# Ordering the recurrence's gate products in a hybrid attention and recurrent layer: a fixed place, a fixed alternation, and an early sigmoid

## The chip, the cores and the metric

The kernel runs on one core of one Trainium2 chip. A core has a matrix engine (PE, TensorE), whose weight loads are shown as an engine of their own (PEld), and four other engines: DVE (VectorE), ACT (ScalarE), POOL (GpSimd) and SP (SyncE, which here issues DMA transfers). Each engine works through its own list of instructions in order, and waits for another engine through semaphores. The metric is the device time of one execution in microseconds (us). Less is better. Where several timed executions of a kernel are given, their median is compared.

## The reference

One decoder layer, 1024 tokens with 16 learned meta tokens ahead of them, 1024 features, all in float32. The input is normalised, and one projection gives five parts: queries, keys and values of an attention with a window of 128 tokens, and two inputs, x and y, of a recurrence over 512 channels. The two results are joined and projected out, normalised and added to the input; a feed-forward part with squared ReLU follows, again normalised and added.

The part that matters here is the recurrence. After a causal convolution of x over 4 tokens:

```python
xb = x.reshape(bsz, t, LRU_BLOCKS, LRU_BLOCK)          # 8 blocks of 64 channels
gate_r = einsum("btnc,ncd->btnd", xb, w_a) + b_a
gate_i = einsum("btnc,ncd->btnd", xb, w_x) + b_x
r, i = sigmoid(gate_r), sigmoid(gate_i)
log_a = -LRU_C * r * softplus(-lam)
a = exp(log_a);  mult = sqrt(-expm1(2 * log_a))
h_t = a_t * h_(t-1) + mult_t * i_t * x_t
rec = gelu(y) * h
mix = concat([attention, rec]) @ w_out
```

So the gates are products with small block-diagonal matrices, of 64 by 64 each; each sigmoid needs its whole gate product; the exponential, the square root and the scan over time follow the sigmoids; and the output projection needs the attention for its first 512 input features and the recurrence for the other 512.

## The kernel before

Every float32 matrix product is done as three products of numbers cut to a shorter mantissa: each operand is split into a high part (a cast, on ACT, line 96) and a low part (the rest, a subtraction on DVE, line 99), and high by high, high by low and low by high are summed in one PSUM bank. The function `mm3` (lines 125, 130, 131) issues the three. A product of 128 rows by 512 columns is the common case.

The kernel goes through the layer in this order. It projects keys, values and the first queries. It then runs eight steps of attention (`scores` and `attend`, four pairs of blocks of tokens for each of two groups of heads). Ten further projections, the `fills` (queries, x and y of the recurrence), give PE products to run while the softmax and the splits go on elsewhere: eight are emitted one a step, with a priority lowered by `FILL_LAG`, and the last two, the y projections of channel blocks 2 and 3, behind the gates in the source (the products L125, L130 and L131 into a bank `ps_acc` that the trace shows between the gates are such projections). After the attention come the gates of the four channel blocks, 128 channels each; then the rest of the recurrence in two halves, blocks 0 and 1 and then blocks 2 and 3; then the output projection, the norm and the feed-forward part.

The gates (`gates(c)`) work as follows. A block of 128 channels holds two of the reference's blocks of 64. Each gate product uses 64 of PE's 128 rows: for s = 0 the one half of the rows, for s = 1 the other. The 1040 tokens go in three thirds of 348, 348 and 344 columns. For each third there are two PSUM banks, one for each s, taken in turn from three rings of banks (`s`, `pt`, `o`), and six matmuls, three for each s (line 819). So a block has 18 gate matmuls and the four blocks 72. Two sigmoids a third (through `lut`, line 82) read the banks into z. The rings are shared with other work: the `o` banks are the value banks of `attend` (matmuls of line 697, read by a copy on ACT, line 706, and an addition on DVE, line 707), and a bank is free for its next use only when its readers are done.

Behind the gates, `gather` (lines 833 to 836) puts the halves together and multiplies by x; `decay` takes exponentials and tanh; `recur` takes a square root and then two multiplications and a scan on DVE (lines 851, 852, 853); `rec_out` (line 858) multiplies by gelu(y) and splits the result into the operands of the output projection, `at[half][2]` for blocks 0 and 1 and `at[half][3]` for blocks 2 and 3. `split_wo` splits the output weights. `out_mm` then runs the output projection, eight input chunks kc of 128 features: kc 0 to 3 read the attention, kc 4 and 5 the recurrence's blocks 0 and 1, kc 6 and 7 its blocks 2 and 3. Later, `u2_tiles` transposes a normalised tile of tokens on PE (line 1003) and scales it out of PSUM (ACT line 1014, DVE line 1008); `combine` (line 1029) forms the sums and differences that the feed-forward's fast matrix scheme multiplies; line 96 splits them.

The order in which an engine runs its instructions isn't that of the source. A list scheduler takes the whole program, with priorities by place in the source and a model of times, and writes out one list for each engine. Three helpers bind it by order alone, without a semaphore: `lut` chains every table function on ACT in source order, because a change of function set costs a table load (line 82, ACT_TABLE_LOAD); `chained` does the same for chosen splits; and `behind(name, ins)` makes one instruction come after another in the order:

```python
def behind(name, *inss):
    for ins in inss:
        tc.add_manual_dep(ins, name, mybir.DependencyInfo(
            mybir.DependencyClass.NoSync, mybir.DependencyReason.DATA), reason="order")
```

Nothing binds the gate matmuls before the change: the scheduler puts each where it finds it ready.

Of the kernel before, what the change touches and what calls it, by code (L numbers as in the profile page):

```python
# [9 lines left out]
F32 = mybir.dt.float32  # L10
F32R = mybir.dt.float32r
AF = mybir.ActivationFunctionType
ALU = mybir.AluOpType
# [3 lines left out]
P = 128  # L17
# [20 lines left out]
def hybrid_layer(  # L38
# [6 lines left out]
    nc = tc.nc  # L45
# [4 lines left out]
    small = ctx.enter_context(tc.tile_pool(name="small", bufs=4))  # L50
# [4 lines left out]
    bufs = {"raw": 2, "ws": 5, "a": 16, "b": 17, "c": 8, "d": 4, "e": 2}  # L55
    uid = [0]

    def slot(tag, shape, dt=F32):
        uid[0] += 1
        return slab.tile(shape, dt, tag=tag, name=f"{tag}{uid[0]}", bufs=bufs[tag])  # L60

    def pair(tag, shape):
        return slot(tag, shape, F32R), slot(tag, shape, F32R)

    def bank(tag, shape=(P, 512)):
        uid[0] += 1
        return ps.tile(list(shape), F32, tag=tag, name=f"ps_{tag}{uid[0]}")

    def f32(ap):
        return ap.bitcast(F32)  # L70
# [8 lines left out]
    last_lut = [None]  # L79

    def lut(*args, **kwargs):
        ins = nc.scalar.activation(*args, **kwargs).ins
        if last_lut[0] is not None:
            tc.add_manual_dep(
                ins, last_lut[0],
                mybir.DependencyInfo(
                    mybir.DependencyClass.NoSync, mybir.DependencyReason.DATA
                ),
                reason="lut",
            )  # L90
        last_lut[0] = ins.name
        return ins

    def split(hi, lo, src, eng=None):
        if eng is None:
            nc.scalar.copy(hi, src)  # L96
        else:
            eng.tensor_copy(hi, src)
        low = nc.vector.tensor_tensor(lo, src, f32(hi), op=ALU.subtract).ins  # L99
        mark[0] = low.name  # L100
        return low
# [4 lines left out]
    def behind(name, *inss):  # L106
        for ins in inss:
            tc.add_manual_dep(
                ins, name,
                mybir.DependencyInfo(  # L110
                    mybir.DependencyClass.NoSync, mybir.DependencyReason.DATA
                ),
                reason="order",
            )
# [69 lines left out]
    eps_col = const.tile([P, 1], F32, name="eps_col")  # L184
# [346 lines left out]
    for h in range(2):  # L531
        r, o, m = HALF[h], HALF[1 - h], slice(P - NMETA, 2 * P)
# [77 lines left out]
    def scores(jp, quarter):  # L610
# [57 lines left out]
            )  # L668
        return sn

    def attend(jp, quarter, sn):
        flat = sn.rearrange("p a b c -> p (a b c)")
        pp = []
        for h in range(2):

            ph, pl = (slot("c", [P, 4, 2, P], F32R) for _ in range(2))
            pt = bank("pt")
            for i in range(4):
                nc.tensor.transpose(pt[:, i * P : (i + 1) * P], sn[:, h, i, 0:P], ident)
            pt = pt.rearrange("p (a b) -> p a b", a=4)  # L680
            split(ph[:, :, 0], pl[:, :, 0], pt)
            for p_ in (ph, pl):
                for s, g, op in ((1, 1, ALU.is_ge), (0, -1, ALU.is_gt)):
                    nc.gpsimd.affine_select(  # L684
                        out=p_[:, :, s], in_=f32(p_[:, :, 0]), pattern=[[0, 4], [g, P]],
                        compare_op=op, fill=0.0, base=0, channel_multiplier=-g,
                    )
            pp.append((ph, pl))
        kb0 = 2 * quarter
        for h in range(2):  # L690
            po = bank("o")
            two = po.rearrange("p (j c) -> p j c", j=2)
            for n, (oc, pc, w) in enumerate(((0, 0, P), (0, P, 2 * P), (P, 3 * P, P))):
                kb = kb0 + n
                v = vk[h][:, kb - 1, :] if kb else vm[:, h, :]
                for k, p_ in enumerate(pp[h]):
                    nc.tensor.matmul(  # L697
                        two[:, :, oc : oc + w], v,
                        p_.rearrange("p (j i) s c -> p j (i s c)", j=2)[:, :, pc : pc + w],
                        start=n == 0 and k == 0, stop=n == 2 and k == 1,  # L700
                        skip_group_check=True,
                    )

            r, o = HALF[h], HALF[1 - h]
            whole = flat[r, 0:512]
            nc.scalar.copy(whole, po[o, :])
            nc.vector.tensor_tensor(whole, po[r, :], whole, op=ALU.add)
        ah, al = at[quarter // 2][jp]
        c = slice(256 * (quarter % 2), 256 * (quarter % 2) + 256)
        split(  # L710
            ah[:, :, c], al[:, :, c],
            flat[:, 0:512].rearrange("p (j c) -> p j c", j=2),
        )
# [65 lines left out]
    for jp in range(2):  # L779
        at_pair(jp)  # L780
        for quarter in range(4):
            gate_after = last_lut[0]
            sn = scores(jp, quarter)
            with deferred(FILL_LAG):
                next_fill()
            if prev is not None:
                attend(*prev)
            prev = (jp, quarter, sn)
    attend(*prev)


# [10 lines left out]
    nc.vector.tensor_tensor(gw[:, 1], graw, f32(gw[:, 0]), op=ALU.subtract)  # L802

    rg = [None] * NLRU

    def gates(c):
        ch, cl = pair("b", [P, TT])
        split(ch, cl, xc[c])


        z = [slot("c", [P, TT]) for _ in range(2)]
        for t0, n in THIRDS:
            acc = []
            for s in range(2):
                flip[0] += 1
                acc.append(bank(("s", "pt", "o")[flip[0] % 3]))
            for k, (a, b) in enumerate(((0, ch), (0, cl), (1, ch))):
                for s in range(2):
                    nc.tensor.matmul(
                        acc[s][:, :n], gw[HALF[s], a, c, :], b[HALF[s], t0 : t0 + n],  # L820
                        start=k == 0, stop=k == 2, skip_group_check=True,
                    )
            for s in range(2):
                lut(
                    z[s][:, t0 : t0 + n], acc[s][:, :n], AF.Sigmoid,
                    bias=prm[:, c, 5 + s : 6 + s],
                )
        rg[c] = z
# [51 lines left out]
    for c in range(NLRU):  # L880
        gates(c)
        if c < 2:
            gather(c)
# [75 lines left out]
    def out_banks(t):  # L959
        tag = ("pt", "o", "acc", "s", "pt", "acc", "s", "pt")[t]  # L960
        return [bank(tag), bank(tag)]
# [201 lines left out]
    for t in range(8):  # L1163
        po = pos[t] if t < 4 else out_banks(t)
# [396 lines left out]
```

## Time and profile before

| | |
|---|---|
| median of 3 runs | 950.23 us (949.52 to 950.42) |
| profiled execution | 949.03 us |
| its span in the trace | 947.3 us |
| mean granted clock of PE | 0.998 |
| PE busy | 937.9 us, 99% of the span |
| DVE, ACT, POOL busy | 664.4, 505.0, 135.9 us |
| chain that ended last | PE 97%, DVE 1% |
| gate matmuls on PE | from 193.49 to 213.16 us |
| sigmoids on ACT | 24, from 197.31 to 214.58 us |

The table's rows are averages over stages that differ. A row of the timeline gives a start in us from the start of the span, a duration in us, the engine, the line of the kernel, the operation, the tile written and the tiles read, the shape, and how many such instructions were merged into the row; square brackets give how long the engine had been idle before it and what ended that. On PE matmuls overlap in the pipe: the duration of one (0.39 us) is longer than the distance to the next (0.23 us), so costs on PE are taken from distances between starts.

### The profile page before, as it was taken

The numbers are of one execution on the slowest core, as the hardware profiler recorded it, in microseconds if no ns is written. First come the engines' busy times: TensorE is split into PE (matmuls) and PEld (weight loads), VectorE is DVE, ScalarE is ACT, GpSimd is POOL, SyncE is SP. The second block draws the span as 40 slices with busy tenths as digits, with TensorE's granted clock in tenths as the row PEclk, the third lists the DMA queues.
The fourth block names the chain that finished last, engine by engine and source line by source line (L and its number), as shares of the span: only waits on it lengthen the run. The fifth ranks groups of instructions, "written<-read, shape, count | busy, mean of one in ns | idle before, by whom it ended". The sixth has DMA issues, their size and how long they took to land.

```text
span 947.3 us, 12174 instructions
## 1 busy us (share of the span) xinstructions
PE 937.9 (99%) x4584; PEld 784.8 (83%) x4584; DVE 664.4 (70%) x849; ACT 505.0 (53%) x844; POOL 135.9 (14%) x205
## 2 busy tenths in 40 slices
PE   9999999999999999999999999999999999999996
PEld 8999999878888878888888888888888888888885
DVE  6667788779977987665544465476667676779783
ACT  8546765569634664443655575654533443445441
POOL 4104437431021100010000000001111000001201
PEclk9999999999999999999999999999999999999999
DMA  8220011104259658574422363334777655537934
GB/s 273 57 68 23 24 45 45 45 23 141 82 194 273 200 180 283 188 258 134 156 89 89 111 215 120 109 111 114 198 170 178 206 179 192 194 126 209 238 64 89
DMA packets 97366, 134.91 MB, mean 142 GB/s; under 512 B 22230, under 2 KB 61158, under 8 KB 97308
## 3 DMA queue, kind: packets, MB, share of 16 engines
q1 hardware_dynamic: 87996, 108.64, 35.3%
q0 software_dynamic: 8880, 24.19, 11.9%
q10 hardware_dynamic: 432, 1.31, 0.4%
q8 instruction: 36, 0.59, 0.3%
q14 instruction: 22, 0.18, 0.1%
HBM read 112.55 MB, written 20.97 MB: 141 GB/s over the span
## 4 chain that ended last, share of the span: by engine, by line
PE 97%; DVE 1%; DMA 0%; ACT 0%; issue 0%; SPq 0%; DVEq 0%
PE ps_acc L125 12%; PE ps_acc L131 12%; PE ps_acc L130 12%; PE ps_pt L131 6%; PE ps_s L131 6%; PE ps_pt L125 6%; PE ps_pt L130 6%; PE ps_s L125 6%; PE ps_s L130 6%; PE ps_o L125 5%; PE ps_o L131 5%; PE ps_o L130 5%; PE ps_o L697 2%; PE ps_acc L282 1%; PE ps_s L629 1%; PE ps_s L633 1%
## 5 line engine op out<-in xcount | busy, mean ns | idle before, releaser
L99 DVE TENSOR_TENSOR ws<-raw,ws 128x1024 fp32r<-128x1024 f32 (+1 forms) x69 | 82.3, 1193 | 72.4 <-PE ps_o L130 23.1
L96 ACT CAST ws<-raw 128x1024 fp32r<-128x1024 f32 (+1 forms) x68 | 69.8, 1027 | 82.0 <-PE ps_o L130 33.6
L96 ACT CAST ws<-e 128x1024 fp32r<-128x1024 f32 x41 | 43.0, 1050 | 85.8 <-PE ps_o L130 38.2
L130 PE MATMUL ps_acc<-a,ws 128*128 128x512 f32 (+3 forms) x240 | 82.9, 346 | 0.0
L125 PE MATMUL ps_acc<-a,ws 128*128 128x512 f32 (+3 forms) x240 | 82.8, 346 | 0.0
L131 PE MATMUL ps_acc<-a,ws 128*128 128x512 f32 (+3 forms) x240 | 82.2, 343 | 0.0
L99 DVE TENSOR_TENSOR b<-b,b 128x1024 fp32r<-128x1024 f32 (+2 forms) x50 | 59.0, 1179 | 27.9 <-PE ps_o L130 22.6
L99 DVE TENSOR_TENSOR ws<-e,ws 128x1024 fp32r<-128x1024 f32 x41 | 50.2, 1223 | 31.7 <-ACT ws L96 18.4
L96 ACT CAST b<-b 128x1024 fp32r<-128x1024 f32 (+2 forms) x49 | 50.0, 1020 | 41.8 <-DVE b L1029 35.5
L684 POOL TENSOR_SCALAR_AFFINE_SELECT c<-c 128x512 fp32r<-128x512 f32 x64 | 55.0, 873 | 73.7 <-ACT c L96 64.2
L125 PEld LDWEIGHTS ps_acc<-a,ws 128*128 128x128 f32 x240 | 45.2, 189 | 4.3 <-issue 0.7
L131 PEld LDWEIGHTS ps_acc<-a,ws 128*128 128x128 f32 x240 | 45.2, 188 | 3.7 <-issue 0.2
L130 PEld LDWEIGHTS ps_acc<-a,ws 128*128 128x128 f32 x240 | 45.2, 188 | 3.6 <-issue 0.4
L131 PE MATMUL ps_acc<-ws,b 128*128 128x512 f32 (+1 forms) x120 | 46.3, 386 | 0.0
L130 PE MATMUL ps_acc<-ws,b 128*128 128x512 f32 (+1 forms) x120 | 46.2, 385 | 0.0
L125 PE MATMUL ps_acc<-ws,b 128*128 128x512 f32 (+1 forms) x120 | 46.0, 385 | 0.0
L125 PE MATMUL ps_pt<-ws,b 128*128 128x512 f32 x112 | 44.3, 395 | 0.0
L131 PE MATMUL ps_pt<-ws,b 128*128 128x512 f32 x112 | 44.2, 395 | 0.0
L130 PE MATMUL ps_pt<-ws,b 128*128 128x512 f32 x112 | 44.1, 394 | 0.0
L131 PE MATMUL ps_s<-ws,b 128*128 128x512 f32 x110 | 43.4, 394 | 0.0
L130 PE MATMUL ps_s<-ws,b 128*128 128x512 f32 x110 | 43.4, 394 | 0.0
L125 PE MATMUL ps_s<-ws,b 128*128 128x512 f32 x110 | 43.3, 394 | 0.0
(417 smaller groups left out, 2660.0 us busy)
## 6 DMA issues: line engine op xcount, KB each, us to landing
raw<-in_w_ff_dram SPq DMA_DIRECT2D x59, 512.0 KB, 3.9
e<-in_w_ff_dram SPq DMA_DIRECT2D x43, 512.0 KB, 3.5
a<-in_w_ff_dram SPq DMA_DIRECT2D x12, 512.0 KB, 6.0
s_dram<-a POOLq DMA_DIRECT2D x12, 512.0 KB, 4.1
raw<-in_w_in_dram SPq DMA_DIRECT2D x9, 512.0 KB, 3.6
c<-in_x_dram SPq DMA_DIRECT2D x8, 512.0 KB, 4.5
d<-in_x_dram SPq DMA_DIRECT2D x8, 512.0 KB, 3.4
out_dram<-raw SPq DMA_DIRECT2D x8, 512.0 KB
```

The source lines that it names most:

```text
L96: nc.scalar.copy(hi, src)
L99: low = nc.vector.tensor_tensor(lo, src, f32(hi), op=ALU.subtract).ins
L125: ins = nc.tensor.matmul(dst, lh, rh, start=start, stop=False, skip_group_check=True).ins
L130: nc.tensor.matmul(dst, lh, rl, start=False, stop=False, skip_group_check=True)
L131: last_mm[0] = nc.tensor.matmul(dst, ll, rh, start=False, stop=stop, skip_group_check=True).ins.name
L282: last_mm[0] = nc.tensor.matmul(acc[:, :n], w[k // 2][:, kc, :], u[kc][k % 2][:, t0 : t0 + n], start=k == 0 and kc == 0, stop=k == last an ...
L629: nc.tensor.matmul(dst, q[h][:, c], hi, start=True, stop=False, skip_group_check=True,)
L633: nc.tensor.matmul(dst, q[h][:, c], lo, start=False, stop=True, skip_group_check=True,)
L684: nc.gpsimd.affine_select(out=p_[:, :, s], in_=f32(p_[:, :, 0]), pattern=[[0, 4], [g, P]], compare_op=op, fill=0.0, base=0, channel_multip ...
L697: nc.tensor.matmul(two[:, :, oc : oc + w], v, p_.rearrange("p (j i) s c -> p j (i s c)", j=2)[:, :, pc : pc + w], start=n == 0 and k == 0, ...
```

## The change

Three edits, all of order. First, `attend` notes its last DVE addition, which is the last read of a value bank, and the first gate matmul of block 0 is ordered behind it; the first gate matmul of each later block is ordered behind the last sigmoid of the block before. Second, every other gate matmul is ordered behind the one ahead of it in the source, so that the two s alternate: 0, 1, 0, 1. Third, a sigmoid of a single column, whose result nobody reads, is emitted ahead of the gates; it enters the chain of table functions. No operation of the computation is changed.

```diff
+    drained = [None]
+
     def attend(jp, quarter, sn):
...
             nc.scalar.copy(whole, po[o, :])
-            nc.vector.tensor_tensor(whole, po[r, :], whole, op=ALU.add)
+            drained[0] = nc.vector.tensor_tensor(
+                whole, po[r, :], whole, op=ALU.add
+            ).ins.name
...
     rg = [None] * NLRU
+    warm = small.tile([P, 1], F32, name="warm", tag="warm", bufs=1)
+    lut(warm, eps_col, AF.Sigmoid)
 
     def gates(c):
         ch, cl = pair("b", [P, TT])
         split(ch, cl, xc[c])
+        start = last_lut[0] if c else drained[0]
...
             for k, (a, b) in enumerate(((0, ch), (0, cl), (1, ch))):
                 for s in range(2):
-                    nc.tensor.matmul(
+                    ins = nc.tensor.matmul(
                         acc[s][:, :n], gw[HALF[s], a, c, :], b[HALF[s], t0 : t0 + n],
                         start=k == 0, stop=k == 2, skip_group_check=True,
-                    )
+                    ).ins
+                    if start:
+                        behind(start, ins)
+                    start = ins.name
```

## Prediction

> **What bounds the kernel now.** I read the page first, then PE's timeline around the gates, then ACT's and DVE's over the recurrence, then all three in the last tile of tokens.
>
> ```profile
> span 947.3 us, 12174 instructions
> PE 937.9 (99%) x4584; PEld 784.8 (83%) x4584; DVE 664.4 (70%) x849; ACT 505.0 (53%) x844; POOL 135.9 (14%) x205
> ...
> PE 97%; DVE 1%; DMA 0%; ACT 0%; issue 0%; SPq 0%; DVEq 0%
> ```
>
> PE is busy for 99% of the span and is 97% of the chain that ended last. So a PE product saved is time saved, and a wait put in front of PE is time lost, unless something later already makes PE wait. The question is then what PE's new order costs it.
>
> ```profile
> 193.17:213.42 20.25, 20.25 (x117) 14.39 (x116) 14.32 (x18) 13.40 (x26) 5.28 (x4) 1.00 0.11 27
> ```
>
> ```profile
> 193.17 0.39 PE L125 MATMUL ps_acc<-a,ws 128*128 128x512 f32 x1
> ...
> 195.86 1.09 PE L697 MATMUL ps_o<-c,b 128*128 128x256 f32 x5
> ...
> 200.61 0.39 PE L130 MATMUL ps_acc<-a,ws 128*128 128x512 f32 x1
> 200.84 0.40 PE L131 MATMUL ps_acc<-a,ws 128*128 128x512 f32 x1
> 201.16 0.43 PE L819 MATMUL ps_s<-b,e 64*128 64x348 f32 x1
> 201.17 0.42 PE L819 MATMUL ps_o<-b,e 64*128 64x344 f32 x1
> 201.43 0.32 PE L819 MATMUL ps_s<-b,e 64*128 64x348 f32 x1
> ...
> 201.59 0.32 PE L819 MATMUL ps_s<-b,e 64*128 64x348 f32 x1
> ...
> 212.84 0.32 PE L819 MATMUL ps_o<-b,e 64*128 64x344 f32 x1
> 213.08 0.50 PE L131 MATMUL ps_acc<-a,ws 128*128 128x512 f32 x1
> 213.42 0.39 PE L125 MATMUL ps_acc<-a,ws 128*128 128x512 f32 x1
> ```
>
> The first row is the stretch of the gates: its length, then each engine's busy time and count, PE first, then the granted clock, here 1.00. Three things are seen in the timeline. Ordinary 512-column products are 0.23 apart (200.61 to 200.84). Two gate matmuls on different halves of the rows start together (201.16 and 201.17), and the next pair follows 0.16 later (201.43 to 201.59). And each change between the two kinds costs time: 0.32 into the first pair instead of 0.23 (200.84 to 201.16), 0.27 to the second instead of 0.16 (201.16 to 201.43), 0.24 out of the last instead of 0.16 (212.84 to 213.08), and 0.34 from the first ordinary one to the second instead of 0.23 (213.08 to 213.42). Together a run of gate matmuls costs 0.09 + 0.11 + 0.08 + 0.11 = 0.39 us beside its pairs.
>
> **The change part by part.** The built order of PE's list says where the 72 gate matmuls stand. Before, they lie in nine runs of 3, 1, 3, 5, 3, 24, 18, 3 and 12, mixed with the last products of `attend`. After, all stand behind those, in four runs of 25, 11, 18 and 18, with 13, 19 and 19 ordinary products between and 21 behind the last one ahead of the output projection, where there were 48. The number of instructions on PE is the same.
>
> The early sigmoid. It adds one column on ACT, and its table load lies in idle time in front of the gates:
>
> ```profile
> 196.01 1.28 ACT L82 ACT_TABLE_LOAD   x1 [3.86 <-PE ps_s L819]
> ...
> 197.88 0.58 ACT L706 COPY c<-ps_o 64x512 f32<-64x512 f32 x1
> 198.48 1.06 ACT L96 CAST b<-b 128x1040 fp32r<-128x1040 f32 x1
> ...
> 214.02 0.56 ACT L82 ACTIVATE c<-ps_o,prm 128x344 f32<-128x344 f32 x1
> 214.60 1.28 ACT L82 ACT_TABLE_LOAD   x1
> ...
> 234.07 1.28 ACT L82 ACT_TABLE_LOAD   x1
> ...
> 254.78 0.62 ACT L96 CAST b<-b 128x512 fp32r<-128x512 f32 x1 [6.20 <-DVE b L858]
> ```
>
> The load (1.28) fits in 3.86 idle, so it costs nothing; if that cover were gone, it would cost the first sigmoid 1.28, which only lengthens the wait in the first run of gates, within the bound given there.
>
> Gates on PE. Between 193.17, an ordinary product just before the first gates, and 213.42 stand, of the 117 in the row of the stretch, the 72 gate matmuls, 38 ordinary ones (38 x 0.231 = 8.78 us) and six value products of L697 (about 0.9 by the row of five). That leaves 20.25 - 8.78 - 0.9 = 10.6 us for the gates. After: 36 pairs x 0.16 = 5.8, four runs x 0.39 = 1.6, together 7.3, a gain of 3.2. Part of it goes into waits. The first run takes 25 matmuls, and the seven of block 1 in it need banks that block 0's first sigmoids give back. The first sigmoid then stands in ACT's list behind the last copy of L706 and two casts of L96 (a large one and the one of the attention's result). I chain these from PE's last value product, which after the change ends at about 196.5, by the durations in these rows (0.58, 1.06 and, for 512 columns, 0.62; each overlaps the next a little): first sigmoid at 198.75, its bank free at 199.3. PE, which starts the run at 197.4 and needs 9 pairs for block 0, is there at 198.8 and waits 0.5, and again 0.3 for the next. With the odd singles I take 1.0 off: **-2.2 us**, bounds -3.2 (no waits) and -1.0 (waits double).
>
> The sigmoids come later. Nothing of the gates is dropped, but the last run now has 21 ordinary products behind it and not 48: 27 more are ahead of it, 27 x 0.231 = 6.2 us, of which the gain of 2.2 is taken off: the last gates run about 4.1 us later (217.0 in place of 212.84), and the last sigmoid ends at 219.1 in place of 214.58. In ACT's list one large cast (0.96 to the next) now stands between it and the table load for the exponentials, at 220.0 in place of 214.60: +5.4. From there I went through ACT's and DVE's lists in their new order with the durations of before. Casts of the output weights have moved from the stretch behind the gelus into that of the exponentials, so the second table load for exponentials (blocks 2 and 3) comes at 240.6 instead of 234.07 (+6.5), but behind it fewer casts are left, and the last scans start 4.0 later than the 249.63 of before.
>
> ```profile
> 249.63 4.54 DVE L853 TENSOR_TENSOR_SCAN c<-b,b 128x1040 f32<-128x1040 f32 x2
> ...
> 257.68 0.39 PE L125 MATMUL ps_pt<-a,b 128*128 128x512 f32 x1
> ...
> 258.60 0.39 PE L130 MATMUL ps_pt<-a,b 128*128 128x512 f32 x1
> 259.02 0.50 PE L131 MATMUL ps_pt<-a,b 128*128 128x512 f32 x1
> ```
>
> Before, the first cast of `at[0][3]` ends at 254.78 + 0.62 = 255.4 and PE comes to the products with kc 6 and 7 at 257.68, with a wait of only 0.19 within (258.60 to 259.02 instead of 0.23). So there were 2.3 us between cast and use. After, PE arrives 2.2 earlier, at 255.5, and the cast starts 4.1 later, at 258.9, and ends at 259.5. PE waits there about 4.0 us, with 0.3 more for kc 5 ahead of it and the old 0.19 gone: **+4.1 us**. The list of PE has only output products behind these matmuls, with the same operands, so nothing can fill it. Bounds: 0 if the chain through ACT and DVE comes only 0.1 later than before (2.2 earlier and 2.3 spare), and 5.0 if it is late by the whole 5.4 of the table load.
>
> The last tile. The scheduler's list differs also far behind: in the stage of the last tile twelve products into a `pt` bank, with three into an `s` bank, stood behind the last eight transposes (L1003) and now stand ahead of them.
>
> ```profile
> 331.99 1.03 PE L1003 MATMUL ps_o<-ident,d 128*128 128x128 f32 x8
> 332.78 0.48 PE L125 MATMUL ps_s<-b,b 128*128 128x512 f32 x1
> ...
> 333.56 0.39 PE L125 MATMUL ps_pt<-b,a 128*128 128x512 f32 x1
> ...
> 336.35 0.39 PE L125 MATMUL ps_acc<-b,e 128*128 128x512 f32 x1
> ...
> 345.13 0.48 PE L125 MATMUL ps_s<-b,e 128*128 128x512 f32 x1
> 345.45 0.40 PE L130 MATMUL ps_s<-b,e 128*128 128x512 f32 x1
> 345.92 0.51 PE L131 MATMUL ps_acc<-b,e 128*128 128x512 f32 x1
> ```
>
> ```profile
> 332.63 1.14 ACT L1014 ACTIVATE c<-ps_o,gcol 128x128 f32<-128x128 f32 x4 [0.93 <-PE ps_o L1003]
> ...
> 334.25 2.61 ACT L96 CAST b<-a 128x1024 fp32r<-128x1024 f32 x4
> ```
>
> ```profile
> 333.07 0.76 DVE L1008 TENSOR_TENSOR c<-ps_o,gcol 128x256 f32<-128x256 f32 x2
> 333.74 0.42 DVE L1029 TENSOR_TENSOR a<-c,c 128x256 f32<-128x256 f32 x1
> ```
>
> From the transposes' start to the cast of their sums is 334.25 - 331.99 = 2.26 us, and of the four casts the next `acc` product needs the first large and the first small one, half of 2.61. Before, fifteen products (332.78 to 336.35, 3.6 us) covered that. After, PE goes from the transposes, which take 0.79 (331.99 to 332.78), straight to the `acc` product: 2.26 + 1.3 - 0.79 = 2.8 us of waiting, and 0.2 for the slow start behind a wait; against it the waits of before at 345.45 and 345.92 go (0.09 + 0.24 above the 0.23). **+2.7 us**; bounds 0 (the `acc` product needs none of these casts) and 3.2.
>
> The rest (SP's list issues some weights a few places earlier or later, ACT's issue of a transfer of the norm weights stands between the sigmoids of blocks 1 and 2) I put at nothing: PE has ordinary products until those operands are read, and if a transfer came late its wait would add to one of the two above. POOL's list is unchanged.
>
> Sum: -2.2 + 4.1 + 2.7 = +4.6 us on the profiled 949.03, 953.6. The median of before lies 1.2 above its profiled execution; the change put on the median gives 950.23 + 4.6 = **954.8 us**.
>
> **The rivals.** A, faster: the recurrence isn't late. Its place is the cast at 254.78, its price is the 4.1, and it decides if the chain comes within 0.1 us of its old time, so that the scheduler's move of the weight casts gives back all of the 5.4. With the last tile's chain covered as well (if the product that I read as waiting needs only older casts) only the gates stay: 950.23 - 2.2 = 948.0. Against it: ACT was idle only 6.20 in front of that cast, and it waited there for DVE, whose own chain starts at the square roots. B, one wait of the two: only the recurrence's gives 950.23 - 2.2 + 4.1 = 952.1; only the last tile's, 950.7. The first is likelier, as the last tile's order is far from the change and reading its chain is less safe. C, the clock: a wait of 4 us is new to PE in this stage, where the trace of before shows none over 0.5.
>
> ```profile
> 939.89 0.28 PE L131 MATMUL ps_acc<-a,b 128*128 128x256 f32 x1
> ```
>
> ```profile
> 943.00:944.00 1.00, 0.00 (x0) 0.00 (x0) 0.26 (x1) 0.00 (x0) 0.00 (x0) 0.85 1.03 207
> 944.00:947.30 3.30, 0.00 (x0) 0.00 (x0) 0.00 (x0) 0.00 (x0) 0.00 (x0) 0.50 0.44 161
> ```
>
> The last matmul ends at 940.17, and the granted clock (the number ahead of the last two) falls to 0.50 at about 943.7, as its mean of 0.85 over 943 to 944 says: 3.5 us of idleness halve it. A wait of 4.0 can reach that. If the clock then stays at half for as long as it took to fall, 3.5 us of work take 1.75 longer: 956.5. What brings it back no row of this case shows. The Trainium skill, "TensorE: Matmul & The Clock Gate", Part 1, says that one idle window of about 3.4 us brings the half clock and one busy window of the same length the full one, and that the window runs free: the trace agrees on the fall. By that page a gap of 4.0 holds a whole window in about (4.0 - 3.4) / 3.4, some 2 times in 10, which is an estimate, and costs 1.7.
>
> D, no effect: the alternation buys nothing where pairs ran already (201.16 and 201.17), the runs' number doesn't matter, and the waits are small: 950.2.
>
> **How the numbers follow.** Forecast with both waits at full clock 0.60; C 0.13; B with the recurrence's wait alone 0.08, with the last tile's alone 0.03; A 0.11; D 0.05. Apart from no change a measurement of this kernel can tell about 0.2%, 1.9 us. Faster is A: 0.11, with a little of the forecast's misses 0.12. Within 0.2% (948.3 to 952.1) are D, the last tile's wait alone and half of B: 0.12. Slower is the rest: 0.76. The forecast's own range goes from 952.4 (waits 1.5 shorter, gates -3.2 and some of the last tile gone) to 956; with B at its foot and C with both bounds at its head the range is 950.6 to 957.6, which leaves out A, part of D and little else.
>
> **What would show it.** Gates: four runs of L819 with the last starting near 215.6, and the output projection reaching its first product about 2 us earlier. Sigmoids: the table load for exponentials near 220. Recurrence: a PE gap of about 4 us near 256, ended by ACT's cast L96 behind DVE L858. Last tile: a PE gap of about 3 us near 338, behind eight transposes. Clock: matmuls some 0.46 apart (twice the 0.23) for a few us behind the gap near 256. Wrong would make it above all that PE comes to kc 6 and 7 and finds the operand there, or that the gap near 338 is missing.

## The result, and the profile after

The changed kernel takes 960.23 us (median of 4 executions, 959.22 to 961.11) against 949.93 us for the kernel before: a ratio of 1.0109, 95% interval 1.0096 to 1.0122. It is slower by 10.3 us, more than twice the forecast of 4.6, and above the range. The profiled execution is the one of 959.22 us. Its page:

```profile
span 957.5 us, 12179 instructions
...
PE 940.1 (98%) x4584; PEld 785.9 (82%) x4584; DVE 664.8 (69%) x849; ACT 504.9 (53%) x845; POOL 135.4 (14%) x205
...
PE 89%; DVE 3%; ACT 3%; DMA 2%; issue 1%; SPq 1%; DVEq 0%
```

PE has the same 4584 matmuls, but it is 89% of the chain that ended last and not 97%: DVE, ACT and a transfer have come into it. PE's waits (what it waited for; us in total, times, longest) name the two places:

```profile
PE ps_pt L125 <- ACT b L96: 3.6, 1, 3.6
PE ps_acc L125 <- ACT b L96: 2.6, 1, 2.6
```

Both traces have the same number of matmuls, so the start of the k-th one in each (counted from 0) can be compared. This table gives how far the changed kernel is behind at chosen places, by the time of that place before:

| matmul | at, before | behind by | added since the row above | what lies between |
|---|---|---|---|---|
| 200th | 29.8 us | +1.87 | +1.9 | start: projections on the first tokens |
| 1240th | 187.1 | +1.82 | 0 | attention |
| 1434th | 224.9 | -0.42 | -2.2 | the gates |
| 1560th | 254.0 | -0.13 | +0.3 | output projection, kc 0 to 5 |
| 1640th | 272.7 | +5.05 | +5.2 | first use of kc 6 and 7, and behind it |
| 1860th | 321.6 | +5.06 | 0 | output projection |
| 1960th | 342.8 | +9.44 | +4.4 | the last tile |
| 2010th | 354.8 | +9.01 | -0.4 | feed-forward |
| 2040th | 361.8 | +10.06 | +1.05 | feed-forward |
| last | 939.9 | +10.04 | 0 | the rest |

The two large rows hold more than the waits. Here are windows of the changed kernel (length; busy time and count of PE, PEld, DVE, ACT, POOL; then the granted clock, the share of the transfers and GB/s):

```profile
257.70:261.35 3.65, 0.01 (x1) 0.00 (x1) 3.65 (x5) 0.67 (x2) 0.00 (x0) 1.00 0.00 0
261.35:262.00 0.65, 0.65 (x3) 0.56 (x4) 0.65 (x2) 0.65 (x2) 0.00 (x0) 1.00 0.00 0
262.00:265.00 3.00, 3.00 (x9) 2.34 (x8) 3.00 (x6) 1.90 (x4) 0.00 (x0) 0.51 0.08 14
265.00:266.00 1.00, 1.00 (x4) 0.81 (x4) 1.00 (x2) 0.00 (x0) 0.00 (x0) 0.77 0.92 332
341.60:344.20 2.60, 0.00 (x1) 0.00 (x1) 2.19 (x8) 2.13 (x6) 0.00 (x0) 0.96 0.98 296
344.20:347.20 3.00, 3.00 (x7) 2.35 (x8) 3.00 (x6) 2.97 (x4) 0.00 (x0) 0.50 0.12 43
```

Behind each wait the granted clock is at half for 3.4 us. The first time it falls 0.7 us after PE has begun to work again, the second time while PE still waits. Matmuls are then 0.43 apart and not 0.23: about 1.6 us lost each time. So the +5.2 is 3.6 of waiting and 1.6 of clock, and the +4.4 is 2.6 of waiting, 0.2 of the slow start behind it and 1.6 of clock.

### The profile page after: what moved, and what is told of

Read it like the earlier page. It is cut to its first block, busy times and chain, and to the rows that moved or that the text cites. A ratio compares the mean times of both kernels' runs of the same rounds, so it can differ in the third digit from the quotient of the medians.

```text
span 957.5 us, 12179 instructions
## 1 busy us (share of the span) xinstructions
PE 940.1 (98%) x4584; PEld 785.9 (82%) x4584; DVE 664.8 (69%) x849; ACT 504.9 (53%) x845; POOL 135.4 (14%) x205
## 3 DMA queue, kind: packets, MB, share of 16 engines
q10 hardware_dynamic: 432, 1.31, 0.4%
## 4 chain that ended last, share of the span: by engine, by line
PE 89%; DVE 3%; ACT 3%; DMA 2%; issue 1%; SPq 1%; DVEq 0%
PE ps_acc L125 11%; PE ps_acc L130 11%; PE ps_acc L131 11%; PE ps_pt L125 6%; PE ps_pt L130 6%; PE ps_pt L131 6%; PE ps_s L131 6%; PE ps_s L125 6%; PE ps_s L130 6%; PE ps_o L130 5%; PE ps_o L125 5%; PE ps_o L131 5%; PE ps_o L699 2%; DMA c<-in_x_dram 1%; ACT c L82 1%
```

## The experiments

All with the comparison kernel, the kernel before, timed on the same chip (949.1 to 949.3 us there).

**The changed kernel again.** No edit.

> The changed kernel once more. Theory: of its +10.3 us, -2.2 come from the gates, +4.0 and +2.5 from the two waits near 259 and 343 us, and +1.6 each from the half clock behind them, all of which repeat; the +1.8 that PE is late by 27 us, before anything that the change touches, and the +0.9 near 354 us are transfers that came late in that execution. If so, this trace shows both waits and both half-clock stretches again, but PE's place at 27 us may be another one, and the time is 957.5 to 960. Rival: the late start belongs to the program, and PE is again 1.8 us late there: 960.

Median 958.80 us (957.11 to 960.40), a ratio of 1.0105 (1.0088 to 1.0122). In its trace PE is 0.93 behind at the 200th matmul where the first trace had 1.87; from there on the two run in parallel: -2.2 over the gates, a wait of 3.63 and half clock, a wait of 2.62 and half clock, +1.1 near 362. In the traces of the other variants below, the 200th matmul is between 0.03 and 1.31 behind, and in all traces each engine runs the same instructions in the same order up to 180 us. So the late start varies from one execution to the next with the same lists; it isn't an effect of the change. The +1.1 near 362 came back: it is one.

**Does idle time halve the clock? Work put into the wait.** A float32 product by a block of zeros, which adds nothing to the result, N times between kc 5 and kc 6 of the first tile (the mask `above`, no longer needed, is set to zero for it):

```diff
+    nc.gpsimd.memset(above, 0.0)
...
+                if t == 0 and n == 0 and kc == 6:
+                    late = idle_mm(po[0], wo[5][0][:, 0:512], N)  # N matmuls, lhsT = above
                 mm3(
                     po[n], (ah[:, kc % 2, s], al[:, kc % 2, s]),
-                    (wo[kc][0][:, c], wo[kc][1][:, c]), kc == 0, kc == KC - 1,
+                    (wo[kc][0][:, c], wo[kc][1][:, c]), kc == 0, kc == KC - 1, late,
                 )
```

PE's list up to there is the same for every N, with the gates in four runs of 18. N = 1 and N = 6:

> The changed kernel with one product by a block of zeros (float32, nothing is added to the result) between the products of kc 5 and those of kc 6. It is the control for the next: a PE wait of about 4.5 us or more stays in front of kc 6, and behind it matmuls lie 0.43 apart for about 3.4 us (half clock), a loss of about 1.6.

> The same with six such products in the place of one, about 0.9 us each; PE's order up to there is the same. Theory (the idle time halves the clock): PE's idle time in front of kc 6 falls below 1.5 us, the matmuls behind it lie 0.23 apart from the first on, and PE is about 1.6 us earlier than with one such product some 40 us later. Rival (something else lowers the clock there, the burst of work or its power): the half clock is still seen and both are level.

N = 4 and N = 5:

> Four float32 products by zeros between kc 5 and kc 6 (one left about 4.7 us idle, six left 0.4). About 2.0 us stay idle. If only an idle time of 3.5 us halves the clock, as at the end of the program, none is seen behind it; if a shorter one does, by the runs so far from about 1.5 us on and not each time, half clock for about 3 us follows.

> Five such products: about 1.1 to 1.3 us stay idle. No half clock behind it by either reading.

One execution each, read by their traces. The wait in front of kc 6 is 4.7 us with one, 2.1 with four, 1.2 with five and 0.4 with six. The windows from 262 on, first with four products, then with five:

```profile
262.00:263.00 1.00, 0.84 (x3) 0.70 (x4) 1.00 (x3) 1.00 (x3) 0.00 (x0) 0.78 0.00 0
263.00:264.00 1.00, 1.00 (x4) 0.81 (x3) 1.00 (x3) 1.00 (x3) 0.00 (x0) 0.50 0.00 0
264.00:265.00 1.00, 1.00 (x4) 0.71 (x4) 1.00 (x3) 0.71 (x2) 0.00 (x0) 0.50 0.00 0
265.00:266.00 1.00, 1.00 (x4) 0.81 (x3) 1.00 (x3) 0.00 (x0) 0.00 (x0) 0.51 0.40 94
```

```profile
262.00:263.00 1.00, 1.00 (x5) 0.83 (x6) 1.00 (x3) 1.00 (x3) 0.00 (x0) 1.00 0.00 0
263.00:264.00 1.00, 1.00 (x6) 0.79 (x5) 1.00 (x2) 1.00 (x3) 0.00 (x0) 1.00 0.00 0
264.00:265.00 1.00, 1.00 (x6) 0.75 (x4) 1.00 (x3) 0.38 (x1) 0.00 (x0) 1.00 0.00 0
265.00:266.00 1.00, 0.95 (x5) 0.53 (x4) 1.00 (x3) 0.08 (x1) 0.00 (x0) 1.00 0.77 233
```

With 2.1 us idle the clock is halved for some 3 us, with 1.2 it isn't (nor with six products; with one it is, from 262.7 on). From the 1434th to the 1640th matmul, the added ones not counted (each product is two records of 0.43 us in the trace), PE falls behind by 7.6 us with one and with four of them, and by 6.3 and 6.8 with five and six. Of the 6.8, 0.5 is a wait for a low part that only the run with six has there. What is left is a step of 1.3 us exactly where the half clock goes, though the operand that PE waits for comes at the same time in all four (within 0.1 us, each trace's own start taken off). The idle time is the cause. A threshold of 3.5 us is refuted. The times of the whole, 959.41, 957.31, 957.36 and 958.91 us with one, four, five and six, don't follow this order, because what comes behind differs too: with six, a half clock comes near 366 instead, behind waits of 0.8 and 1.1 us.

**The last tile: the transposes' place.** The twelve products bound behind the last transposes, where they stood before the change (`turned[0]` is the last transpose's name):

```diff
-    p2(2, a12_early[2])
+    p2(2, a12_early[2], turned[0])
```

> The changed kernel with the twelve products of the last tile put behind the last eight transposes again, as they were before the change. The prediction's step (the transposes' place uncovers the chain): the wait near 343 us goes, and with it the half clock behind it, -2.6 - 1.6, 956. Rival (DVE's list ends the wait: DVE works without a pause on sums and low parts that now stand ahead of the last four sums, and the transposes' place only matters to PE's own order): PE waits as long as in the changed kernel, for the same cast at the same time, and the time is 960.

Median 958.40 us (957.50 to 959.57), a ratio of 1.0099 (1.0084 to 1.0114): as slow as the changed kernel. The transposes now run at 336.16 and not at 340.54; PE comes to that stage 1.6 us less late, so 2.8 of it is the bind. PE waits all the same. In this kernel's timelines of PE, ACT and DVE:

```profile
336.16 1.03 PE L1015 MATMUL ps_o<-ident,d 128*128 128x128 f32 x8
...
342.53 0.80 PE L125 MATMUL ps_acc<-b,e 128*128 128x512 f32 x1 [2.56 <-ACT b L96]
```

```profile
341.13 2.60 ACT L96 CAST b<-a 128x1024 fp32r<-128x1024 f32 x4 [2.46 <-DVE a L1043]
```

```profile
339.08 0.75 DVE L1022 TENSOR_TENSOR c<-ps_o,gcol 128x256 f32<-128x256 f32 x2
...
340.68 0.75 DVE L1043 TENSOR_TENSOR a<-c,c 128x256 f32<-128x256 f32 x2
```

The transposes are done by 337.2, but DVE scales their result out of PSUM only at 339.08 and forms the sums at 340.68 (lines 1022 and 1043 here are 1008 and 1029 of the kernel before), and ACT sits idle for 2.46 us until then. DVE itself has no idle time from 334.68 to 342.1: other sums, low parts and additions stand ahead in its list. In this kernel the order that the scheduler wrote for DVE ends the wait, not the place of the transposes. In the changed kernel both limits come at almost the same time. These are rows of its ACT:

```profile
341.18 1.14 ACT L1024 ACTIVATE c<-ps_o,gcol 128x128 f32<-128x128 f32 x4 [0.90 <-PE ps_o L1013]
342.80 2.61 ACT L96 CAST b<-a 128x1024 fp32r<-128x1024 f32 x4 [0.47 <-DVE a L1039]
```

There ACT does wait for the transposes, and the cast starts 342.80 - 340.54 = 2.26 us behind their start, just what the prediction's chain takes. With the transposes 2.8 us earlier the cast comes only 0.1 us earlier, PE's lag taken off: DVE's list holds it.

**Which edit does it.** Four variants. Alternation alone (`start = None` at each block, no early sigmoid):

> The kernel before with the alternation inside each block alone: no place for the first gate matmul, no early sigmoid. Theory: the loss comes from the places (the first gates behind the last value bank's read and each block behind the sigmoids of the one before), which spread the gates and push the last sigmoids back; the alternation moves little. PE's list then has the gates in eight runs, the last at 212, and only waits of about 1 us at kc 6 and 7, too short for the half clock: +0.5 to +2.5 us over before. Rival: the alternation itself spreads the gates; then the wait at kc 6 is 3 us or more and the time is 6 us or more over before.

The places alone (`start = None` behind each block's first gate matmul, no early sigmoid):

> The kernel before with the places alone (first gate matmul of block 0 behind the last value bank's read, that of each later block behind the last sigmoid of the block before), no alternation, no early sigmoid. Only the first matmul of a block is bound, the others lie where the scheduler finds room. Theory: the last block's gates come later still than in the changed kernel (near 219 to 220), so PE waits twice around kc 6 (about 1 and 2.2 us) and again in the last tile (2.6): +8 to +11 us over before. Rival (the alternation is what hurts): 0 to +2.

The changed kernel without the order behind the sigmoids:

```diff
-        start = last_lut[0] if c else drained[0]
+        start = None if c else drained[0]
```

> The changed kernel without the order of blocks 1 to 3 behind the sigmoids of the block before; block 0's place, the alternation and the early sigmoid stay. Theory: the last gates come 1 to 2 us earlier and with them the sigmoids; the wait at kc 6 falls from 3.6 to below 1.5 us, and no half clock follows it; the last tile's wait of 2.5 us stays, with half clock behind it: +4 to +6 us over before, some 4 to 5 less than the changed kernel. Rival (the wait at kc 6 is set by something other than the sigmoids' place): it stays above 3 us and the time is that of the changed kernel.

Alternation and that order, but block 0 not placed. The expectation says that this kernel has no early sigmoid; the kernel that ran has it, so it differs from the alternation alone in two edits and from the changed kernel in one:

```diff
-        start = last_lut[0] if c else drained[0]
+        start = last_lut[0] if c else None
```

> The kernel before with the alternation, and blocks 1 to 3 placed behind the last sigmoid of the block before; block 0 isn't placed and there is no early sigmoid. It is the alternation-only kernel plus that place alone. Theory: that place is what costs most: waits of about 2.2 us (kc 5) and 1.1 us (kc 6) and of 2.6 us in the last tile, and half clock behind at least two of them: +7 to +10 us over before, 957 to 960. Rival (block 0's place behind the last value bank's read is needed for the loss): below +3.

| kernel | median, us | ratio to before (95%) | PE's waits over 0.5 us past 190 us | stretches at half clock |
|---|---|---|---|---|
| alternation alone | 951.09 | 1.0018 (1.0009 to 1.0028) | 0.5, 0.9 | 0 |
| places alone | 961.76 | 1.0130 (1.0115 to 1.0145) | 1.5, 0.5, 1.9, 2.8 | 3 |
| changed, not behind the sigmoids | 954.24 | 1.0050 (1.0033 to 1.0066) | 0.6, 2.6 | 1 |
| alternation, behind the sigmoids, early sigmoid | 956.09 | 1.0075 (1.0059 to 1.0092) | 1.5, 0.8, 2.6, 0.8 | 0 |
| changed | 960.23 | 1.0109 (1.0096 to 1.0122) | 3.6, 2.6, 0.6 | 2 |

The alternation alone costs 0.2% and brings the gates nothing (PE is 0.1 us less behind after them than ahead of them). Taking the order behind the sigmoids out of the changed kernel brings the wait at kc 6 from 3.6 down to 0.6 and saves 0.6%; adding it, with the early sigmoid, to the alternation costs 0.6%, nearly all of it in the last tile (3.1 us) and near 362 (1.2), as around kc 6 the gates' gain of 1.4 pays for the wait. How late the recurrence is can be read from the cast of `at[0][3]`, each trace's own start taken off: it starts at 254.8 before, at 256.5 with the alternation alone, at 256.7 in the changed kernel without the order behind the sigmoids, at 258.6 with the alternation and that order, and at 258.9 in the changed kernel. Of the 4.1 us, the alternation alone thus makes 1.7, and the place of the blocks behind the sigmoids 2.1 to 2.2. The places alone lost 12.4 us, more than the 8 to 11 expected. The expectation for the kernel with the alternation behind the sigmoids, half clock behind two waits, was wrong: in its profiled execution none is seen, not even behind 2.6 us of idleness, though its loss of 7.0 us lies at the foot of the limits expected:

```profile
338.70:341.30 2.60, 0.06 (x1) 0.06 (x1) 2.17 (x7) 2.19 (x6) 0.00 (x0) 1.00 1.09 375
341.30:345.00 3.70, 3.70 (x15) 2.85 (x16) 3.70 (x6) 3.62 (x5) 0.00 (x0) 1.00 0.93 296
```

And in the kernel with the places alone 1.5 us were enough, with the fall 0.5 us behind the wait (a mean of 0.81 over 0.8 us is half clock in the last 0.3):

```profile
201.70:203.20 1.50, 0.01 (x1) 0.01 (x1) 1.49 (x3) 1.49 (x3) 0.00 (x0) 1.00 0.31 63
203.20:204.00 0.80, 0.80 (x4) 0.80 (x5) 0.80 (x2) 0.80 (x3) 0.00 (x0) 0.81 0.87 236
204.00:207.00 3.00, 3.00 (x13) 2.43 (x12) 2.63 (x5) 3.00 (x8) 1.21 (x1) 0.50 0.29 81
```

**Both causes taken back.** The changed kernel, not behind the sigmoids, and with the bind of the last tile:

> The same, and the twelve products of the last tile bound behind the last transposes. In this order DVE's list has the last sums early, so both theories let the wait near 340 us fall to about 1 us, short of the half clock: +0.5 to +2.5 us over before. If the time is 3 us or more over before, a loss is left that neither the waits nor the clock explain.

Median 952.81 us, a ratio of 1.0036 (1.0022 to 1.0049): +3.5, more than expected. No wait is longer than 0.8 us and no half clock is seen. Its trace gives the rest: -1.1 over the gates, +0.9 around kc 6, +1.9 in the last tile (several short waits), +1.3 near 362. The last comes, as in the changed kernel, behind a late transfer of feed-forward weights, which I had not counted. Here the same bind as above, in another order of DVE's list, does cut the last tile's wait, from 2.6 to below 0.7: in that order the transposes' place sets it.

**The early sigmoid.** The changed kernel without it:

> The changed kernel without the early one-column sigmoid. Theory: the table load (1.28 us) now stands behind ACT's last copies and casts, directly in front of the first real sigmoid, so the wait inside the first run of gates grows by about 1.3 us (from 0.15 beside the pitch to about 1.5) and everything behind is 1.3 later: +1 to +1.5 us over the changed kernel, 960 to 962. Rival (ACT has time for the load anyway, as the prediction priced it): the same time as the changed kernel.

Median 959.88 us (958.75 to 962.64), a ratio of 1.0118 (1.0100 to 1.0136) where the changed kernel on that scale has 1.0105 and 1.0109. In the trace the wait in the first run of gates is 1.59 us (`PE ps_s L824 <- ACT c L82`) and not 0.15, and the gates' gain falls from 2.2 to 0.8. In the time of the whole, a difference of 1.3 us can't be told from the spread of these kernels; the trace shows it at its place. No kernel here beats the one before.

## Why the prediction was wrong, point by point

*Gates on PE, -2.2.* Right: -2.2 in each of three traces with this order (after, again, and with the last tile's bind). Four runs of 25, 11, 18 and 18. The wait in the first run is there; two distances of 0.47 and 0.44 in place of 0.16 make it some 0.6 us, where 0.8 was foretold (a row of the changed kernel's PE, whose bracket counts only the time that PE is empty):

```profile
201.13 0.42 PE L826 MATMUL ps_s<-b,e 64*128 64x348 f32 x1 [0.15 <-ACT c L82]
```

*The early sigmoid costs nothing.* Right, and without it the first run waits 1.4 us longer, as its stated alternative said.

*The sigmoids come later, +4.1.* Right in its chain and its size. All times of this trace carry the 1.8 us of the late start:

```profile
220.50 0.57 ACT L82 ACTIVATE c<-ps_o,prm 128x344 f32<-128x344 f32 x1
220.93 1.08 ACT L96 CAST a<-d 128x1024 fp32r<-128x1024 f32 x1
222.03 1.28 ACT L82 ACT_TABLE_LOAD   x1
...
242.51 1.28 ACT L82 ACT_TABLE_LOAD   x1
...
260.68 0.62 ACT L96 CAST b<-b 128x512 fp32r<-128x512 f32 x1 [5.39 <-DVE b L868]
```

Less 1.8, the table loads stand at 220.2 and 240.7 and the cast at 258.9; foretold were 220.0, 240.6 and 258.9. PE waits 3.64 us, with 0.3 more ahead of it.

*The last tile, +2.7.* The size was right (2.62 of waiting and a slow start), and the chain from the transposes is there (2.26 us to the cast, as foretold); but it isn't the only one. The step said that the transposes' new place uncovers the chain; with the place restored in the changed kernel the wait stays, as DVE's list alone makes the cast as late. Only in the kernel without the order behind the sigmoids does the place alone decide. DVE's list had to be followed, not only PE's. In the changed kernel DVE's scaling of the tile that the transposes read starts at

```profile
336.28 0.74 DVE L1001 TENSOR_SCALAR d<-raw,rs 128x1024 f32<-128x1024 f32 x1
```

which, less the 5.1 that PE is behind there, is 331.2; before, it was 326.76.

*The rest, put at nothing.* Wrong by +1.05 - 0.4 = 0.6. The chain of the changed kernel goes through a transfer of feed-forward weights that is issued behind DVE's late sums and takes 8.06 us (start, us, what):

```profile
353.68 8.06 DMA a<-in_w_ff_dram
```

DVE and ACT then split it just too late, and PE waits near 366. Why this order makes the transfer late, and not only as late as PE itself, wasn't taken apart by a run.

*The clock, rival C.* This is the step that failed. The prediction read a threshold, "3.5 us of idleness halve it", from the end of the program, where nothing comes after the last matmul. That 3.5 was luck: in the 14 traces the fall comes between 2.0 and 5.2 us behind the last matmul (4.7 in the changed kernel). It held the 2.8 us wait harmless and the 4.0 one harmless in most cases, and gave C 0.13. In fact both waits halved the clock in both profiled executions of the changed kernel. The price, 1.75 for each, was nearly right (1.6); there were two. 3.2 us of the missing 5.7 are these.

*The base.* The sum was put on one profiled execution of before, as if every execution began alike. The first 30 us vary by up to 1.9 between executions, and the profiled one of the changed kernel has nearly all of that. That is another 1.8 between the two traces; between the medians it is less, and how much can't be read from the times.

Forecast and trace: -2.2 + 4.1 + 2.7 = 4.6 foretold; -2.2 + 3.9 + 2.8 for the same terms as measured, + 3.2 clock + 0.6 transfers + 1.8 start = 10.1.

## What to carry to other kernels

On a kernel whose PE is never idle, price a new wait of PE at its length and the half clock behind it, 1.3 to 1.6 us here, as soon as it is about 2 us long, and look for the clock in the windows behind the wait, not inside it. A dependency that gathers small products into neat runs can save what it promised on PE (2.2 us) and lose more, when the last of them now comes behind work that used to follow it. A scheduler's lists change far from the edit: read all engines' lists there, since PE's wait may be set by a list in which the visible difference doesn't lie, or by two at once.

## What the runs showed of the hardware that I had not expected

The half clock needs no long idleness. Over the traces of the changed kernel and of the experiments, it came behind 14 of 15 single waits of PE of 2.1 us and more (the miss is one of 2.56); behind two of the five between 1.5 and 1.9 (1.5 and 1.9, and not behind 1.5, 1.6 and 1.7); never behind a single one below 1.3; and once behind 0.8 and 1.1 in short succession. It begins between 0.7 us before and 1.0 us after PE has resumed, and lasts 3.41 us, once twice that.

The length of a wait doesn't decide alone, and the traces show what else does. Each trace records when the granted clock changes, and within a trace the falls lie whole steps of 3.413 us apart, whatever PE does: in the changed kernel at 262.05, 343.97 and 954.96 us, which are 24 and 179 steps. So the clock is set at the ends of steps that run on by themselves. Counted step by step in all 14 traces, up to the last matmul, PE's idle share decides:

| idle share of a step | steps | half clock in the next step |
|---|---|---|
| 0.60 and more | 14 | 14 |
| 0.44 to 0.56 | 6 | 3 |
| below 0.40, at full clock | all others | 0 |

The harmless wait of 2.56 us lay across two steps, with idle shares of 0.55 and 0.20; the harmful one of 1.5 us put 0.44 into one. A harmless one of 1.5 us did so too, so between 0.44 and 0.56 the share that the trace shows doesn't decide it. The same lists can therefore meet the half clock in one execution and miss it in the next. The changed kernel without the order behind the sigmoids fits this: its four executions have mean granted clocks of 0.996, 0.996, 0.996 and 0.999, and the last, at 952.88 us, is the fastest (the others take 953.69 to 955.87).

The Trainium skill, "TensorE: Matmul & The Clock Gate", Part 1, names an idle window of about 3.4 us for the fall and a busy one of the same length for the return. The runs agree on the window's length and on the return, and disagree on the fall: an idle share of 0.60 of a step was always enough. The Trainium skill, "TensorE: Matmul & The Clock Gate", "A second HAM failure mode: psum-queue depth-cycling", says that short idle times between groups of matmuls can make the clock fall too; the one fall behind 0.8 and 1.1 us agrees with that.
